# The small operands' loads of a fused decoder block, put behind its first large loads

## Chip, cores and metric

The kernel runs on one core of a Trainium2 chip. The metric is the time of one execution on the device in microseconds (us), a median over runs.

## What is computed

One decoder layer over 1024 positions of width 1024, in float32. Cut to what matters here:

```python
hn = rms_norm(h, norm1_g)
a_b, a_c, a_h, q, k, v, c_u, c_v = split(hn @ w_in)
y_a = a_b * short_conv(a_c * a_h, conv_w)
y_b = stick_breaking_attention(rms_norm(q, q_norm_g), rms_norm(k, k_norm_g), v)
y_c = spatial_gating(gelu(c_u), gelu(c_v), sgu_norm_g, sgu_w, sgu_b)
h = h + concat(y_a, y_b, y_c) @ w_out
h = h + square(relu(rms_norm(h, norm2_g) @ w_ff1)) @ w_ff2
gate = sigmoid(rms_norm(h, norm3_g) @ w_ple_gate)
h = h + gate * (p @ w_ple_proj)
```

The small operands are `norm1_g`, `norm2_g`, `norm3_g` (g1, g2, g3 in the kernel), `q_norm_g` and `k_norm_g` (gq, gk), `sgu_norm_g` (gs_b, spread over all partitions), `sgu_b` and `conv_w`. The last product, `p @ w_ple_proj`, needs nothing of the layer, so the kernel computes it first and keeps it in DRAM until the end.

## The kernel before

Every operand of a product is split into a high and a low float32r part, and a product of two operands is three matrix products (high x high, high x low, low x high; L161). ACT casts the high part, DVE (at times POOL) subtracts it from the source for the low part (`split`, L135).

The program is written as one stream; a scheduler in the framework sets the order of each engine's instructions, and an engine runs its own in order. What bears on the change is the first 45 us:

- **Loads.** Large loads are issued on SP into seven stage buffers (`stage`, L64). SP issues the next one when a buffer is free, that is, when ACT and DVE have made its parts. The first ones are two halves of pT, each with the first 384 columns of w_ple_proj, then two more of pT, then the rest of w_ple_proj, then blocks of xT and w_vu in turn.
- **Small loads.** `load_const` (L119) issues a load of a small operand on POOL. All eight stand at the start of the program: L124 to L130 and L543 to L546.
- **First products** (L675 to L686). Eight results `pp` of 128 x 1024, each in two halves; a half is six matrix products into one PSUM bank (`pp_ps`). There are two pools of two banks, one for the first halves and one for the second (`wide_bank`, L88). ACT copies a first half out, DVE a second half. POOL then issues the store of the whole result into DRAM (L686). The results lie in four buffers (tag `wt`, L680), so result 4 goes where result 0 was, once result 0's store has landed, and result 6 where result 2 was.
- **Scaling of x** (`normalize`, L217). Block k of xT is scaled by a column of g1: the high part by ACT (L141), the low part by DVE (L142). ACT squares the block as well (L182). This runs beside the first products.
- **Next products** (`gating`, L548). `vu_ps` takes the next bank in turn after the sixteen halves, the one that held the first half of result 6.

POOL's transfers are counted on eight semaphores that are used in turn (DMASW0 to DMASW7). POOL waits, ahead of an issue, until the transfer that used the same semaphore before has landed.

L1057 to L1065 hold an older use of pacing: a copy of two columns on POOL (`pace`) which waits for a tile, with issues placed behind it.

Of the kernel before, what the change touches and what calls it, by code (L numbers as in the profile page):

```python
# [7 lines left out]
F32 = mybir.dt.float32  # L8
# [5 lines left out]
P = 128  # L14
T = 1024
D = 1024
KT = D // P
# [15 lines left out]
def hybrid_block(ctx: ExitStack, tc: tile.TileContext, a: dict):  # L33
# [5 lines left out]
    nc = tc.nc  # L39
    PSUM = bass.MemoryType.PSUM  # L40

    const = ctx.enter_context(tc.tile_pool(name="const", bufs=1))
# [14 lines left out]
    def name(s):  # L57
        n_of[0] += 1
        return f"{s}_{n_of[0]}"

    def slot(s, dt=F32, shape=(P, HT)):
        return sp.tile(list(shape), dt, tag="slot", name=name(s))

    def stage(src, cols=HT, queue=nc.sync):  # L64
        t = stp.tile([P, HT], F32, tag="stage", name=name("stage"))[:, :cols]
        queue.dma_start(t, src)
        return t
# [11 lines left out]
    def half_tmp(s, shape=(P, 256)):  # L79
        return tp.tile(list(shape), F32, tag="half", name=name(s), bufs=3)  # L80

    def bank(pool, s):
        return pool.tile([P, HT], F32, tag=pool.name, name=name(s))
# [11 lines left out]
    def block(t):  # L95

        return t // 4, slice(t % 4 * P, (t % 4 + 1) * P)
# [21 lines left out]
    def load_const(key, shape):  # L119
        t = const.tile(list(shape), F32, name=f"c_{key}")  # L120
        nc.gpsimd.dma_start(t, a[key])
        return t

    g1 = load_const("g1", [P, KT])  # L124
    g2 = load_const("g2", [P, KT])
    g3 = load_const("g3", [P, KT])
    minus_g3 = const.tile([P, KT], F32, name="minus_g3")
    nc.vector.tensor_scalar_mul(minus_g3, g3, -1.0)
    gq = load_const("gq", [P, 1])
    gk = load_const("gk", [P, 1])  # L130


    last_hi, last_power = [None], [None]
# [1 line left out]
    def split(src, hi, lo, scale=None, low=nc.vector):  # L135

        if scale is None:
            last_hi[0] = nc.scalar.copy(hi, src)  # L138
            low.tensor_tensor(out=lo, in0=src, in1=hi, op=ALU.subtract)  # L139
        else:  # L140
            nc.scalar.activation(hi, src, AF.Copy, scale=scale)  # L141
            nc.vector.scalar_tensor_tensor(out=lo, in0=src, scalar=scale, in1=hi,  # L142
                                           op0=ALU.mult, op1=ALU.subtract)

    def load_w(src, cols, low=nc.vector):

        st = stage(src, cols)
        hi = wp.tile([P, 384], F32R, tag="w", name=name("whi"))
        lo = wp.tile([P, 384], F32R, tag="w", name=name("wlo"))
        split(st, hi[:, :cols], lo[:, :cols], low=low)  # L150
        return hi, lo
# [9 lines left out]
    def product(ps, terms, first=True, last=True):  # L161


        for i, ((lh, ll), (rh, rl)) in enumerate(terms):
            nc.tensor.matmul(ps, lh, rh, start=first and i == 0, stop=False)  # L165
            nc.tensor.matmul(ps, lh, rl, start=False, stop=False)  # L166
            done = nc.tensor.matmul(ps, ll, rh, start=False, stop=last and i == len(terms) - 1)  # L167
        return done

    def cols(parts, sl):  # L170
        return parts[0][:, sl], parts[1][:, sl]

    def power_mhalf(out, in_, n):
        last_power[0] = nc.gpsimd.tensor_tensor(out=out, in0=in_, in1=mhalf[:, :n], op=ALU.pow)  # L174
# [42 lines left out]
    def normalize(h):  # L217
        for k in range(KT):
            xt = stage(a["xT"][k * P:(k + 1) * P, half[h]])
            xn[k][h] = pair("xn")  # L220
            split(xt, *xn[k][h], scale=g1[:, k:k + 1])
            square_sum(S1[h], xt, k == 0, nc.vector)
            yield 1
# [19 lines left out]
    def later(units, piece):  # L243

        waiting.append((emitted[0] + units, piece))

    def stream(*gens):
        for g in gens:
            for units in g:
                emitted[0] += units  # L250
                yield units
                while waiting and waiting[0][0] <= emitted[0]:
                    units = waiting.pop(0)[1]()
                    emitted[0] += units
                    yield units
        while waiting:
            yield waiting.pop(0)[1]()
# [85 lines left out]
    def project(pr):  # L343

        wk = [load_w(a["w_qkv"][pr, k], 384, nc.gpsimd if pr and k % 2 == 0 else nc.vector)
              for k in range(KT)]

        QS = [[None, None], [None, None]]

        KH = [[None, None], [None, None]]  # L350
        KL = [[None, None], [None, None]]
        V = [None] * 4
        heads[pr] = QS, KH, KL, V
        for t in range(KT):
            th, ts = block(t)
            if t % 4 == 0:
                for hh, other in enumerate((hi_p, lo_p)):
                    KL[hh][th] = slot("KL", F32R)
                    nc.gpsimd.memset(KL[hh][th][other].bitcast(F32), 0.0)
                for hh in range(2):  # L360
                    QS[hh][th] = slot("QS", F32R)
                    KH[hh][th] = slot("KH", F32R)
            ps = bank(ps_mm, "qkv_ps")[:, :384]
            for k0 in range(0, KT, 2):
                product(ps, [(cols(xn[k][th], ts), wk[k]) for k in (k0, k0 + 1)],
                        k0 == 0, k0 == KT - 2)
                yield 18

            sq = half_tmp("qk_sq", (P, 4, HD + 1))
            nc.scalar.copy(sq[:, :, HD], ms1e[t].broadcast_to([P, 4]))  # L370
            nc.scalar.activation(sq[:, :, :HD], ps[:, :256].rearrange("p (h d) -> p h d", d=HD),
                                 AF.Square, scale=HD ** -0.5)
            ss = small.tile([P, 4], F32, tag="ss", name=name("ss"))
            nc.vector.tensor_reduce(out=ss, in_=sq, axis=AX.X, op=ALU.add)  # L374
            rs = small.tile([P, 4], F32, tag="rs", name=name("rs"))
            power_mhalf(rs, ss, 4)
            if t % 2 == 0:
                qk = tp.tile([P, 2, 256], F32, tag="qk", name=name("qk"), bufs=2)
            nc.vector.tensor_tensor(
                out=qk[:, t % 2].rearrange("p (h d) -> p h d", d=HD),  # L380
                in0=ps[:, :256].rearrange("p (h d) -> p h d", d=HD),
                in1=rs.unsqueeze(2).broadcast_to([P, 4, HD]), op=ALU.mult)
            if t % 2 == 0:
                V[t // 2] = slot("V", F32R, (P, 2, 2, 2, HD))
            v = V[t // 2][:, t % 2]
            split(ps[:, 256:].rearrange("p (h d) -> p h d", d=HD), v[:, :, 0], v[:, :, 1], scale=r1[t])
            if t % 2 == 1:
                later(72, lambda t=t, qk=qk: turn_qk(heads[pr], t, qk))
# [151 lines left out]
    ATTEND = 2 * (72 + 8 * 10 + 72 + 10 * 10 + 80)  # L540


    gs_b = const.tile([P, 256], F32, name="gs_b")  # L543
    nc.gpsimd.dma_start(gs_b, a["sgu_g"].partition_broadcast(P))
    sgb = load_const("sgu_b", [P, 4])
    cw = load_const("conv_w", [P, 2, 3])  # L546

    def gating():  # L548
        wsT = slot("wsT", shape=(P, 4, P))
        nc.sync.dma_start(wsT, a["sgu_wT"])  # L550
# [111 lines left out]
    wple = []  # L662
# [7 lines left out]
    for c0, n in UNITS[1:]:  # L670
        for k in range(2):
            wple[k].append(load_w(a["w_ple_proj"][k * P:(k + 1) * P, c0 * P:(c0 + n) * P], n * P))
    vu_parts = []
    first_half = normalize(0)
    for n in range(KT):  # L675
        next(first_half)
        st = stage(a["w_vu"][n])
        vu_parts.append(pair("vu"))
        split(st, *vu_parts[n])
        pp = at.tile([P, T], F32, tag="wt", name=name("pp"), bufs=4)  # L680
        for h in range(2):
            ps = wide_bank("pp_ps")
            product(ps, [(cols(wple[k][n // 3], slice(n % 3 * P, (n % 3 + 1) * P)), p_parts[k][h])
                         for k in range(2)])
            (nc.vector.tensor_copy if h else nc.scalar.copy)(pp[:, half[h]], ps)
        nc.gpsimd.dma_start(pp_dram[n], pp)  # L686
    for _ in normalize(1):
        pass
    alone = stream(gating(), project(0))
    fill = stream(project(1), project(2), project(3), convolve())  # L690

# [362 lines left out]


    g_sums = dram.tile([4, 4, P, HT], F32, name="g_sums")
    pace = const.tile([P, 2], F32, name="pace")  # L1057
    def gate_sums(i, behind):

        if not 0 <= i < 16:  # L1060
            return
        paced = nc.gpsimd.tensor_copy(pace, behind[:, :2])
        with tc.issue_after(paced.ins):
            block_step(i % 4, lambda to: g_sums[to, i // 4],
                       lambda of: w_block("w_ple_gate", of, i // 4), nc.gpsimd)  # L1065

# [275 lines left out]
```

## Time and profile before

| | us |
|---|---|
| median of 3 runs | 1219.47 (1216.49 to 1220.53) |
| the profiled execution, its time | 1217.19 |
| its span, first to last instruction | 1215.2 |
| PE busy | 1188.7 (98%) |
| DVE busy | 885.7 (73%) |
| ACT busy | 641.6 (53%) |
| POOL busy | 400.5 (33%) |

Times in the trace count from the start of the span. A row of the timeline has the start, the duration, engine, line, operation and tiles, and in brackets how long the engine was idle before it and what ended that. PE is TensorE, DVE VectorE, ACT ScalarE, POOL GpSimd, SP SyncE. Tiles' names leave out numbers, so c_g is g1, g2 or g3. The median lies 2.28 us above the profiled execution, so a difference is reckoned against that execution's own time.

### The profile page before, as it was taken

Reading aid. Unit: us, or ns where it says so; the run is one execution under the profiler, and the core shown is the slowest. Engines: PE = TensorE matmul, PEld = TensorE weight load, DVE = VectorE, ACT = ScalarE, POOL = GpSimd, SP = SyncE. Lnnn points to the kernel's source line nnn. Section 1 sums busy time; section 2 is a strip of 40 time slices with the busy share of each in tenths; the row PEclk is TensorE's granted clock in tenths of the full one; section 3 lists DMA queues with packets and bytes.
Section 4 is the critical chain, followed back from the end, with each engine's and each line's share of the span. In section 5 each row is a group of like instructions: output and inputs, shape, how many; then the busy total and the mean of one; then the engine's idle time right before and its main releaser. Section 6 shows DMA issues by size and latency. Waiting matters only on the chain.

```text
span 1215.2 us, 17769 instructions
## 1 busy us (share of the span) xinstructions
PE 1188.7 (98%) x5852; PEld 1015.5 (84%) x5852; DVE 885.7 (73%) x1302; ACT 641.6 (53%) x1284; POOL 400.5 (33%) x408
## 2 busy tenths in 40 slices
PE   8999999999999999999999999999999999999997
PEld 7899999898878888888888888888888888888886
DVE  7846888888787757877877777787665557753597
ACT  7737777777654355743334343355443444546542
POOL 2324456465342312124553544421023301013412
PEclk9999999999999999999999999999999999999999
DMA  9703359898653786779989989778889985654857
GB/s 300 239 18 102 115 175 278 233 197 160 145 116 79 166 286 194 207 194 266 258 242 271 239 246 264 210 255 273 320 248 314 278 264 170 216 165 108 185 158 208
DMA packets 127964, 254.04 MB, mean 209 GB/s; under 512 B 14496, under 2 KB 22432, under 8 KB 127168
## 3 DMA queue, kind: packets, MB, share of 16 engines
q1 hardware_dynamic: 94992, 168.08, 41.7%
q0 software_dynamic: 27664, 57.05, 25.3%
q10 hardware_dynamic: 5216, 27.79, 6.3%
q8 instruction: 46, 0.75, 0.3%
q14 instruction: 46, 0.38, 0.1%
HBM read 192.30 MB, written 92.80 MB: 235 GB/s over the span
## 4 chain that ended last, share of the span: by engine, by line
PE 84%; DVE 6%; DMA 3%; ACT 3%; issue 2%; POOL 1%; ACTq 0%; SPq 0%; DVEq 0%; POOLq 0%
PE f_ps L811 25%; PE d_ps L811 25%; PE g_ps L811 6%; PE qkv_ps L165 3%; PE qkv_ps L167 3%; PE qkv_ps L166 3%; PE av L494 2%; PE w_tr L476 2%; DVE rem L451 2%; PE vu_ps L167 1%; PE vu_ps L165 1%; PE vu_ps L166 1%; PE o_ps L167 1%; PE o_ps L165 1%; PE o_ps L166 1%
## 5 line engine op out<-in xcount | busy, mean ns | idle before, releaser
L139 DVE TENSOR_TENSOR w_lo<-raw,w_hi 128x512 fp32r<-128x512 f32 x280 | 241.4, 865 | 87.0 <-ACT w_hi L138 85.1
L138 ACT CAST w_hi<-raw 128x512 fp32r<-128x512 f32 x280 | 171.9, 619 | 231.5 <-PE d_ps L811 114.0
L811 PE MATMUL f_ps<-hn_hi,w_hi 128*128 128x512 f32 x448 | 175.2, 392 | 0.0
L811 PE MATMUL f_ps<-hn_hi,w_lo 128*128 128x512 f32 x448 | 174.8, 391 | 0.0
L811 PE MATMUL f_ps<-hn_lo,w_hi 128*128 128x512 f32 x448 | 174.8, 390 | 0.0
L811 PE MATMUL d_ps<-f_hi,w_hi 128*128 128x512 f32 x448 | 174.8, 390 | 0.0
L811 PE MATMUL d_ps<-f_hi,w_lo 128*128 128x512 f32 x448 | 174.3, 389 | 0.0
L811 PE MATMUL d_ps<-f_lo,w_hi 128*128 128x512 f32 x448 | 174.3, 389 | 0.0
L451 DVE TENSOR_TENSOR_SCAN rem<-rem 128x128 f32<-128x128 f32 (+3 forms) x64 | 87.6, 1376 | 19.5 <-ACT rem L446 18.8
L811 PEld LDWEIGHTS f_ps<-hn_lo,w_hi 128*128 128x128 f32 x448 | 84.5, 189 | 17.9 <-issue 0.2
L811 PEld LDWEIGHTS f_ps<-hn_hi,w_hi 128*128 128x128 f32 x448 | 84.5, 189 | 17.9 <-issue 0.2
L811 PEld LDWEIGHTS f_ps<-hn_hi,w_lo 128*128 128x128 f32 x448 | 84.4, 188 | 17.6
L811 PEld LDWEIGHTS d_ps<-f_lo,w_hi 128*128 128x128 f32 x448 | 84.1, 188 | 17.6 <-issue 0.2
L811 PEld LDWEIGHTS d_ps<-f_hi,w_lo 128*128 128x128 f32 x448 | 84.1, 188 | 17.6
L811 PEld LDWEIGHTS d_ps<-f_hi,w_hi 128*128 128x128 f32 x448 | 84.1, 188 | 17.6 <-issue 0.2
L165 PE MATMUL qkv_ps<-whi,xn_hi 128*128 128x384 f32 x256 | 89.6, 350 | 6.8 <-DVE V L142 6.8
L166 PE MATMUL qkv_ps<-wlo,xn_hi 128*128 128x384 f32 x256 | 86.7, 339 | 0.0
L167 PE MATMUL qkv_ps<-whi,xn_lo 128*128 128x384 f32 x256 | 86.6, 338 | 0.0
L139 DVE TENSOR_TENSOR f_lo<-raw,f_hi 128x512 fp32r<-128x512 f32 x112 | 78.1, 728 | 10.1 <-ACT f_hi L138 9.9
L138 ACT CAST f_hi<-raw 128x512 fp32r<-128x512 f32 x112 | 67.1, 620 | 26.0 <-DMA raw<-f_dram 20.9
L797 POOL TENSOR_TENSOR S<-S,sq 128x512 f32<-128x512 f32 x19 | 25.6, 1345 | 160.2 <-ACT sq L873 160.2
L174 POOL TENSOR_TENSOR rs<-ss,mhalf 128x4 f32<-128x4 f32 x32 | 47.5, 1484 | 68.1 <-DVE ss L374 67.3
(247 smaller groups left out, 2707.9 us busy)
## 6 DMA issues: line engine op xcount, KB each, us to landing
raw<-in_w_ff SPq DMA_DIRECT2D x148, 256.0 KB, 4.1
raw<-f_dram SPq DMA_DIRECT2D x112, 256.0 KB, 5.1
raw<-w_sums SPq DMA_DIRECT2D x64, 256.0 KB, 3.7
f_dram<-f SPq DMA_DIRECT2D x48, 256.0 KB, 4.1
f_dram<-t SPq DMA_DIRECT2D x48, 256.0 KB, 3.7
w_sums<-in_w_ff POOLq DMA_DIRECT2D x8, 1024.0 KB, 12.2
w_sums<-w_sums POOLq DMA_DIRECT2D x8, 1024.0 KB, 12.4
raw<-in_w_out SPq DMA_DIRECT2D x28, 256.0 KB, 3.7
```

What stands on the lines that cost most here:

```text
L138: last_hi[0] = nc.scalar.copy(hi, src)
L139: low.tensor_tensor(out=lo, in0=src, in1=hi, op=ALU.subtract)
L165: nc.tensor.matmul(ps, lh, rh, start=first and i == 0, stop=False)
L166: nc.tensor.matmul(ps, lh, rl, start=False, stop=False)
L167: done = nc.tensor.matmul(ps, ll, rh, start=False, stop=last and i == len(terms) - 1)
L174: last_power[0] = nc.gpsimd.tensor_tensor(out=out, in0=in_, in1=mhalf[:, :n], op=ALU.pow)
L451: nc.vector.tensor_tensor_scan(out=back, data0=back, data1=back, initial=1.0, op0=ALU.mult, op1=ALU.bypass)
L476: nc.tensor.transpose(tr[:, n:n + P], wts[i][:, kb * P:(kb + 1) * P], ident)
L494: nc.tensor.matmul(av[:, first * P:], lhs, part[:, o:o + m], start=kb == 0 and part is hi, stop=kb == 2 * g + 1 and part is lo)
L797: return eng.tensor_tensor(out=out, in0=x, in1=y, op=ALU.add)
L811: done = nc.tensor.matmul(bank, l, r, start=first and k == 0 and i == 0, stop=k == len(b) - 1 and i == 2, skip_group_check=True)
```

## The change

The loads of the small operands leave the start of the program. A helper `once` puts a copy of two columns of a given tile on POOL, which waits until that tile is written, and issues what stands under it behind that copy. The load of g1 stands behind the second high part of w_ple_proj; the other seven stand behind result 2 of the first products. The sign change of g3 moves behind the scaling of x, and the older pacing uses the same helper.

```diff
-    g1 = load_const("g1", [P, KT])
-    g2 = load_const("g2", [P, KT])
-    g3 = load_const("g3", [P, KT])
-    minus_g3 = const.tile([P, KT], F32, name="minus_g3")
-    nc.vector.tensor_scalar_mul(minus_g3, g3, -1.0)
-    gq = load_const("gq", [P, 1])
-    gk = load_const("gk", [P, 1])
+    pace = const.tile([P, 2], F32, name="pace")
+
+    def once(behind):
+
+        return tc.issue_after(nc.gpsimd.tensor_copy(pace, behind[:, :2]).ins)
...
-    gs_b = const.tile([P, 256], F32, name="gs_b")
-    nc.gpsimd.dma_start(gs_b, a["sgu_g"].partition_broadcast(P))
-    sgb = load_const("sgu_b", [P, 4])
-    cw = load_const("conv_w", [P, 2, 3])
...
+    with once(wple[1][0][0].bitcast(F32)):
+        g1 = load_const("g1", [P, KT])
...
+        if n == 2:
+            with once(pp):
+                gs_b = const.tile([P, 256], F32, name="gs_b")
+                nc.gpsimd.dma_start(gs_b, a["sgu_g"].partition_broadcast(P))
+                sgb = load_const("sgu_b", [P, 4])
+                gq = load_const("gq", [P, 1])
+                gk = load_const("gk", [P, 1])
+                g2 = load_const("g2", [P, KT])
+                g3 = load_const("g3", [P, KT])
+                cw = load_const("conv_w", [P, 2, 3])
         nc.gpsimd.dma_start(pp_dram[n], pp)
     for _ in normalize(1):
         pass
+    minus_g3 = const.tile([P, KT], F32, name="minus_g3")
+    nc.vector.tensor_scalar_mul(minus_g3, g3, -1.0)
```

How the orders stand, with the semaphores that a row waits for. On POOL, from the last of its early own work to the third result's store (pp_61 is result 2), before:

```order
L114 AFFINE_SELECT below_104<-below_104 128x128 [waits Pool_49]
L121 DMA c_g3_115<-in_g3 128x8
L121 DMA c_gq_119<-in_gq 128x1
L121 DMA c_gk_121<-in_gk 128x1
L544 DMA gs_b_131<-in_sgu_g 128x256
L121 DMA c_sgu_b_133<-in_sgu_b 128x4
L121 DMA c_conv_w_135<-in_conv_w 128x6
L686 DMA pp_dram_137<-pp_41_211 128x1024 [waits DMASW0_49,DVE_49,Activation_49]
L686 DMA pp_dram_137<-pp_51_244 128x1024 [waits DMASW1_49,DVE_49,Activation_49]
L686 DMA pp_dram_137<-pp_61_277 128x1024 [waits DMASW2_49,DVE_49,Activation_49]
```

and now, from the load of g1 on (whose pacing copy stands ahead of it, behind the work of L114):

```order
L121 DMA c_g1_182<-in_g1 128x8
L692 DMA pp_dram_120<-pp_41_197 128x1024 [waits DVE_49,Activation_49]
L692 DMA pp_dram_120<-pp_51_230 128x1024 [waits DVE_49,Activation_49]
L128 COPY pace_111<-pp_61_263 128x2 [waits Activation_49,Pool_49]
L685 DMA gs_b_281<-in_sgu_g 128x256
L121 DMA c_sgu_b_283<-in_sgu_b 128x4
L121 DMA c_gq_285<-in_gq 128x1
L121 DMA c_gk_287<-in_gk 128x1
L121 DMA c_g2_289<-in_g2 128x8
L121 DMA c_g3_291<-in_g3 128x8 [waits DMASW0_49]
L121 DMA c_conv_w_293<-in_conv_w 128x6 [waits DMASW1_49]
L692 DMA pp_dram_120<-pp_61_263 128x1024 [waits DMASW2_49,DVE_49]
```

The store of result 2 stood directly behind that of result 1 and waited for g3's landing (DMASW2). Seven loads now stand between the two; conv_w waits for the store of result 0 (the one that used DMASW1 before it), and the store of result 2 for that of result 1.

On ACT, around the copy of result 6's first half (pp_101), before:

```order
L141 ACTIVATE xn_hi_85_363<-stage_84_361,c_g1_111 128x512
L685 COPY pp_101_409<-pp_ps_102_410 128x512 [waits DVE_49,DMASW2_49,PE_49,Activation_49]
L138 CAST vu_hi_89_372<-stage_88_370 128x512 [waits DMAHW5_49]
L182 ACTIVATE sq_97_400<-stage_94_394 128x512 [waits DMAHW6_49]
L141 ACTIVATE xn_hi_95_396<-stage_94_394,c_g1_111 128x512
L685 COPY pp_111_442<-pp_ps_112_443 128x512 [waits DVE_49,DMASW3_49,PE_49,Activation_49]
L138 CAST vu_hi_99_405<-stage_98_403 128x512 [waits DMAHW7_49]
L141 ACTIVATE xn_hi_105_429<-stage_104_427,c_g1_111 128x512 [waits DMAHW0_49]
```

and now:

```order
L139 ACTIVATE xn_hi_95_397<-stage_94_395,c_g1_182 128x512
L180 ACTIVATE sq_107_434<-stage_104_428 128x512 [waits DMAHW0_49,DVE_49]
L136 CAST vu_hi_99_406<-stage_98_404 128x512 [waits DMAHW7_49]
L139 ACTIVATE xn_hi_105_430<-stage_104_428,c_g1_182 128x512
L681 COPY pp_101_410<-pp_ps_102_411 128x512 [waits DVE_49,DMASW2_49,PE_49,Pool_49]
L136 CAST vu_hi_109_439<-stage_108_437 128x512 [waits DMAHW1_49]
L139 ACTIVATE xn_hi_115_463<-stage_114_461,c_g1_182 128x512 [waits DMAHW2_49]
```

The copies of results 6 and 7 have moved behind the scaling (xn_hi_105) and square of the eighth block, which are the last of the first half of x. On PE, result 7's second half (pp_ps_113), which stood behind 13 products of vu, now stands ahead of all of vu:

```order
L167 MATMUL pp_ps_103_418<-p_hi_21_170,wlo_34_195 128x512
L165 MATMUL vu_ps_148_537<-vu_hi_39_207,xn_hi_36_200 128x512 [waits Activation_49]
L166 MATMUL vu_ps_148_537<-vu_lo_40_208,xn_hi_36_200 128x512
L167 MATMUL vu_ps_148_537<-vu_hi_39_207,xn_lo_37_201 128x512
L165 MATMUL vu_ps_148_537<-vu_hi_49_240,xn_hi_45_231 128x512
```

This was before (the last product of result 6, then vu), and now:

```order
L165 MATMUL pp_ps_113_452<-p_hi_18_147,wlo_31_172 128x512
L163 MATMUL pp_ps_113_452<-p_hi_21_153,whi_33_177 128x512
L164 MATMUL pp_ps_113_452<-p_lo_22_154,whi_33_177 128x512
L165 MATMUL pp_ps_113_452<-p_hi_21_153,wlo_34_178 128x512
L163 MATMUL vu_ps_148_540<-vu_hi_39_193,xn_hi_36_186 128x512 [waits Activation_49]
```

The first vu product waits for ACT in both, and what it waits for is the copy that frees its bank. From about the second vu result on, the order of every engine is the same as before.

More of the change, by code (lines that the diff above doesn't have):

```diff
@@ L1056, in hybrid_block @@
     g_sums = dram.tile([4, 4, P, HT], F32, name="g_sums")
-    pace = const.tile([P, 2], F32, name="pace")
     def gate_sums(i, behind):
@@ L1061, in gate_sums @@
             return
-        paced = nc.gpsimd.tensor_copy(pace, behind[:, :2])
-        with tc.issue_after(paced.ins):
+        with once(behind):
             block_step(i % 4, lambda to: g_sums[to, i // 4],
```

## The prediction

> **What bounds the kernel now.** I read the page first, then the waits of PE, then the stretches by engine, and last the first 35 us in order of time.
>
> ```profile
> span 1215.2 us, 17769 instructions
> PE 1188.7 (98%) x5852; PEld 1015.5 (84%) x5852; DVE 885.7 (73%) x1302; ACT 641.6 (53%) x1284; POOL 400.5 (33%) x408
> ```
>
> PE is the bound: of 1215.2 us it is idle for 26.5. A change among the first loads can only win back PE's idle time near the start. The waits of PE in the first 130 us (total, times, longest) and the busy time of each engine in three stretches say how much that is:
>
> ```profile
> PE pp_ps L165 <- ACT whi L138: 2.5, 1, 2.5
> PE qkv_ps L165 <- DVE V L142: 1.2, 1, 1.2
> 4.50:8.70 4.20, 1.78 (x8) 1.16 (x7) 1.32 (x3) 1.15 (x3) 2.00 (x4) 1.00 0.96 276
> 8.70:28.00 19.30, 19.26 (x85) 15.96 (x86) 17.56 (x31) 16.33 (x31) 2.67 (x5) 1.00 0.97 330
> 28.00:58.00 30.00, 30.00 (x141) 25.01 (x139) 26.72 (x54) 24.56 (x47) 10.19 (x10) 1.00 0.79 274
> ```
>
> There is one gap of 2.5 us, between 4.5 and 8.7, and then none until 58. In the second stretch 85 products take 19.26 us, so one product of 512 columns takes 0.2266 us; I use that below. The gap in order of time (start, duration, idle before):
>
> ```profile
> 1.46 0.68 POOL L121 DMA_DIRECT2D c_g<-in_g  x1
> 5.67 0.61 PE L167 MATMUL pp_ps<-p_hi,wlo 128*128 128x512 f32 x2
> 5.97 0.53 POOL L121 DMA_DIRECT2D c_conv_w<-in_conv_w  x1
> 7.53 0.62 ACT L138 CAST p_hi<-stage 128x512 fp32r<-128x512 f32 x1 [3.00 <-DMA stage<-in_pT]
> 8.18 0.51 ACT L138 CAST whi<-stage 128x384 fp32r<-128x384 f32 x1
> 8.74 0.73 PE L165 MATMUL pp_ps<-p_hi,whi 128*128 128x512 f32 x2 [2.46 <-ACT whi L138]
> ```
>
> PE ends its first six products at 6.28 and waits for the second weight part, which ACT casts from 8.18 to 8.69. ACT had waited 3.00 us for the third load. The first load (issued in the stretch 0.5 to 1.2), the third (1.7 to 2.15) and the chain's row of the fourth, with their times to landing:
>
> ```profile
> stage<-in_pT SPq DMA_DIRECT2D x1, 256.0 KB, 2.7
> ...
> stage<-in_pT SPq DMA_DIRECT2D x1, 256.0 KB, 5.8
> ...
> 2.19 5.97 DMA stage<-in_w_ple_proj
> ```
>
> So the third and fourth loads took 5.8 and 6.0 us where the first took 2.7. POOL issues its eight small loads from 1.46 to 6.50, in just this stretch.
>
> **The eight small loads leave the start.** POOL's issue time costs nothing, before or after: POOL has no other work on the path there. What matters is how much their transfers hold up the large ones. The queues' shares of the 16 engines from 3.5 to 8.2 (q0 is POOL's, q1 SP's), and then from 12 to 16, where q0 carries nothing:
>
> ```profile
> q1 hardware_dynamic: 671, 1.11, 87.1%
> q0 software_dynamic: 112, 0.02, 4.3%
> ...
> GB/s 287 389 410 389 328 328 348 389 348 348 287 164 184 143 123 205 164 82 143 123 225 164 184 164 205 225 287 225 266 369 328 328 369 430 410 430 348 389 307 307
> q1 hardware_dynamic: 614, 1.11, 93.5%
> ```
>
> The least gain is 0.043 x 4.7 = 0.20 us, the time that small packets hold the engines. The most is the whole gap, 2.46: were the fourth load to land after 2.7 us (at 4.9), its cast would end by 5.4, ahead of PE's 6.28. A loss is excluded, since nothing is put ahead of these loads. Between these ends I stay near the lower one: from 12 to 16 SP's queue alone falls to 82 to 225 GB/s for over 1 us, so the loads have slow spells that no small load causes. I take **0.7 us gained**.
>
> [...]
>
> **The load of g1 comes later, just ahead of its first use.** The first use on ACT, a small copy like the new one on POOL, the landing of the first and of the slowest of the three g loads, and a copy out of PSUM on ACT:
>
> ```profile
> 12.69 0.72 ACT L141 ACTIVATE xn_hi<-stage,c_g 128x512 fp32r<-128x512 f32 x1
> L1062 POOL COPY pace<-h x12: 184/514/581, 891.7 to 973.5; 128x2 f32<-128x2 f32 x12
> c_g<-in_g POOLq DMA_DIRECT2D x1, 4.0 KB, 4.6
> ...
> c_g<-in_g POOLq DMA_DIRECT2D x1, 4.0 KB, 6.4
> ...
> 16.03 0.57 ACT L685 COPY pp<-pp_ps 128x512 f32<-128x512 f32 x1
> ```
>
> On the clock of before: the weight part is written at 8.69, the pacing copy takes 0.51, so the issue begins at 9.2 and g1 lands 4.6 to 6.4 later, at 13.8 to 15.6. The scaling at 12.69 wants it, so ACT is held for 1.1 to 2.9 us. Behind it on ACT are the cast of a weight part, two squares, casts, and the copy at 16.03 (third result, first half) that frees a bank. PE asks for that bank after 42 more products, at 8.74 + 42 x 0.2266 = 18.26; the copy ends at 16.60. So 1.66 us of lateness are covered by the PE products of results 0 to 3, and only 0 to 1.2 us can reach PE. I take **0**: 1.1 is the likelier landing.
>
> [...] If ACT did not catch up, that would be rival C.
>
> **The other seven loads stand ahead of the third result's store.** This is where I see the price. Rows: three stores on POOL as issued now, the first two's time to landing (stretches 14 to 15 and 15 to 16), all eight's, then ACT's copy of result 6 and PE's first vu product:
>
> ```profile
> 14.16 0.54 POOL L686 DMA_DIRECT2D pp_dram<-pp  x1 [7.66 <-ACT whi L138]
> 15.74 0.54 POOL L686 DMA_DIRECT2D pp_dram<-pp  x1 [1.04 <-ACT sq L182]
> 19.56 0.53 POOL L686 DMA_DIRECT2D pp_dram<-pp  x1 [3.28 <-ACT vu_hi L138]
> pp_dram<-pp POOLq DMA_DIRECT2D x1, 512.0 KB, 7.1
> ...
> pp_dram<-pp POOLq DMA_DIRECT2D x1, 512.0 KB, 7.8
> ...
> DMA to landing us min/median/max: 6.2/6.6/7.8
> 27.00 0.56 ACT L685 COPY pp<-pp_ps 128x512 f32<-128x512 f32 x1
> 27.91 0.39 PE L165 MATMUL vu_ps<-vu_hi,xn_hi 128*128 128x512 f32 x1
> ```
>
> POOL's row now: second pacing copy (waits for ACT's half of result 2, 16.60), five issues of 0.54 that wait for nothing, g3 (waits for g1's landing), conv_w (waits for the landing of store 0: 14.16 + 7.1 = 21.26), and only then store 2, which waits for the landing of store 1: 15.74 + 7.8 = 23.54. So store 2 slips from 19.56 to 23.54. With 6.2 to 7.8 to land it is done at 29.74 to 31.34, median 30.14. Four buffers hold the results, so ACT's copy of result 6 goes into the buffer of result 2 and waits for that; with 0.56 for the copy the bank is free at 30.7. PE's first vu product takes that bank. PE itself comes to it after all results: eight of two halves of six products, 96 less the first six, so 8.74 + 90 x 0.2266 = 29.13 (result 7's second half, now ahead of vu, included). That makes a stall of 1.6 us, where before there was none: the copy ended at 27.56 and PE went on at 27.91. Everything in this paragraph moves along with whatever the first loads gain, so the stall doesn't shrink with that gain.
>
> ACT has its own way to the same copy, since its row now puts the last scaling and square of the first half ahead of it. From two rows of now and ACT's total wait for xT between 10 and 40:
>
> ```profile
> 30.54 0.72 ACT L141 ACTIVATE xn_hi<-stage,c_g 128x512 fp32r<-128x512 f32 x1
> 31.16 0.62 ACT L182 ACTIVATE sq<-stage 128x512 f32<-128x512 f32 x1
> ACT sq L182 <- DMA stage<-in_xT: 2.9, 4, 1.2
> ```
>
> The scaling ends at 31.26; two copies of 0.56 that stood ahead now stand behind, the square of 0.62 stands ahead: 31.26 - 1.12 + 0.62 = 30.76, so the copy would end at 31.3 and the stall be 2.2. Held-back stores leave the loads more of the engines, and up to 2.9 us of waiting could go, so this way may be shorter. The ends: no stall, if store 2, alone in its queue, lands like the first load (23.54 + 2.7); and 31.34 + 0.56 - 29.13 = 2.8. I take **1.8 us lost**, between the two ways.
>
> No cost elsewhere. The moved operands are used far behind: the earliest, gs_b, at 47.7. The sign change of g3 moves on DVE behind a scaling of the sixth block; it takes 0.16 us, and DVE is not what PE waits for there.
>
> ```profile
> L614 DVE TENSOR_TENSOR vu<-vu,gs_b x8: 409/420/426, 47.7 to 79.8; 128x256 f32<-128x256 f32 x8
> 11.37 0.16 DVE L128 TENSOR_SCALAR minus_g<-c_g 128x8 f32<-128x8 f32 x1
> ```
>
> From there on the instructions stand as before, and PE, the bound, carries any shift to the end.
>
> **Sum.** -0.7 + 0 + 1.8 = +1.1 us. The profiled execution took 1217.19 us with a span of 1215.2, so it should become 1218.3 and 1216.3. The median of the three runs, 1219.47, lies 2.28 above that execution; on it the forecast is 1220.6.
>
> **The rivals.**
>
> - A, the forecast (0.50): small gain at the start, stall at the first vu product. 1220.6.
> - B (0.30): the small loads do hold up the first ones, and the whole gap of 2.46 goes. For it: 5.8 and 6.0 us against 2.7, while the small loads are in flight. Against it: their 4.3%. With the stall of 1.8 that gives -0.7, 1218.8; without a stall -2.46, 1217.0. More than 2.46 is not there to be had.
> - C, the other side (0.13): g1 lands 2.9 us late and ACT, which does the casts, the scalings and half of the copies, does not catch up. Stage buffers then come free late, loads slip with them, and the copy of result 6 ends at 31.3 + 2.9 = 34.2: a stall of 5.1, 1224.6. It becomes decisive once more than 1.5 us of lateness remain at that copy, for then 2.2 + 1.5 passes 3.66. Against it: ACT waits 2.9 us for loads in this stretch, time in which it could catch up.
> - D (0.07): the order is changed, yet neither effect is seen: the first loads land as before and store 2 is early enough. 1219.5.
>
> **How the numbers follow.** About 0.3%, 3.66 us, is what a measurement of this kernel can tell from no change; the three runs themselves span 4.04. A, B and D all lie inside it. Only B's end without a stall together with a low run would read as faster: 0.04. C and a tail of A make slower: 0.14. The rest, 0.82, is no change. The range goes from B's end, 1217.0, up to the loss with no gain, a stall of 2.8 and part of the 1.2 that g1 can cost (+3.5): 1223.0.
>
> **What would show it.** Step one: times to landing of the third and fourth load (5.8, 6.0) and PE's wait before 8.74; a fall below 4 us and a wait under 1 us prove B. Step two: ACT's idle time before the first scaling, ended by the load of g1, about 1 us. Step three: store 2's issue about 8 us behind store 1's, and a PE wait of 1.6 to 2.2 us at the first vu product, ended by ACT's copy of result 6. If that wait is missing, or follows something else, step three is wrong. If the end moves by more than the start does, what I say of everything behind 30 us is wrong.

## The result, and the profile after

| | before | after |
|---|---|---|
| median of 20 runs each, us | 1218.38 (1213.7 to 1222.24) | 1222.07 (1216.57 to 1228.05) |
| profiled execution: time, span | 1217.19, 1215.2 | 1220.75, 1218.7 |
| PE busy | 1188.7 | 1189.9 |

The ratio is 1.0036 with an interval of 1.0022 to 1.0050: the change makes the kernel slower, by 2.7 to 6.1 us. The forecast was +1.1 us, no measurable change; the outcome is the one that had been given 0.14, though the medians, 3.69 us apart, only just pass the 3.66 us that the prediction set for it.

The waits of PE in the first 130 us after the change (total, times, longest) show a new first row:

```profile
PE vu_ps L163 <- ACT pp L681: 3.6, 1, 3.6
PE pp_ps L163 <- ACT whi L136: 1.6, 1, 1.6
PE qkv_ps L163 <- DVE V L140: 1.2, 1, 1.2
```

The gap before the second half of the first products is 1.6 instead of 2.5, and a gap of 3.6 at the first vu product is new. Both in order of time, with POOL's pacing copy and issues between them:

```profile
6.24 0.62 ACT L136 CAST p_hi<-stage 128x512 fp32r<-128x512 f32 x1 [1.83 <-DMA stage<-in_pT]
...
7.17 0.51 ACT L136 CAST whi<-stage 128x384 fp32r<-128x384 f32 x1 [0.32 <-DMA stage<-in_w_ple_proj]
...
7.73 0.73 PE L163 MATMUL pp_ps<-p_hi,whi 128*128 128x512 f32 x2 [1.62 <-ACT whi L136]
...
8.26 0.70 POOL L121 DMA_DIRECT2D c_g<-in_g  x1
...
11.20 0.72 ACT L139 ACTIVATE xn_hi<-stage,c_g 128x512 fp32r<-128x512 f32 x1
...
14.51 0.54 POOL L692 DMA_DIRECT2D pp_dram<-pp  x1 [1.01 <-ACT sq L180]
...
15.50 0.39 POOL L128 COPY pace<-pp 128x2 f32<-128x2 f32 x1 [0.45 <-ACT pp L681]
...
22.22 1.18 POOL L692 DMA_DIRECT2D pp_dram<-pp  x2 [2.48 <-DVE S L181]
...
28.04 0.39 PE L165 MATMUL pp_ps<-p_hi,wlo 128*128 128x512 f32 x1
...
29.74 0.63 ACT L180 ACTIVATE sq<-stage 128x512 f32<-128x512 f32 x1 [1.80 <-DMA stage<-in_xT]
...
30.28 0.60 ACT L136 CAST vu_hi<-stage 128x512 fp32r<-128x512 f32 x1
...
30.79 0.72 ACT L139 ACTIVATE xn_hi<-stage,c_g 128x512 fp32r<-128x512 f32 x1
...
31.41 0.56 ACT L681 COPY pp<-pp_ps 128x512 f32<-128x512 f32 x1
...
32.03 0.80 PE L163 MATMUL vu_ps<-vu_hi,xn_hi 128*128 128x512 f32 x1 [3.60 <-ACT pp L681]
```

The third load is used at 6.24 (7.53 before), and PE's second half begins 1.01 us earlier. The first scaling, at 11.20, has no idle time before it: g1, issued at 8.26, took 2.9 us to land and was there just in time. The third result's store is issued 7.7 us behind the second's. PE ends the first products at 28.43. ACT is idle until the load of the first half's last block lands at 29.7; square, a cast and the scaling follow, and only then, at 31.41, the copy that frees PE's bank.

The gap has a second price, the granted clock: the share of its full clock that PE was given. The busy times of each engine in four stretches (after the length: PE's busy time and count first; the last three numbers are the granted clock, the DMA share and GB/s):

```profile
27.91:31.32 3.41, 0.52 (x3) 0.09 (x1) 1.80 (x4) 1.61 (x4) 0.00 (x0) 1.00 1.04 383
31.32:34.73 3.41, 2.70 (x6) 2.15 (x7) 3.30 (x6) 2.48 (x6) 0.53 (x1) 0.50 1.01 350
34.73:38.14 3.41, 3.41 (x9) 2.64 (x8) 3.15 (x6) 3.41 (x7) 0.53 (x1) 0.50 1.04 372
38.14:41.55 3.41, 3.41 (x16) 2.82 (x15) 0.27 (x1) 1.54 (x3) 0.00 (x0) 1.00 0.75 284
```

Behind the stretch in which PE worked for 0.52 us only, the clock is at 0.50 for two stretches of 3.41 us, with 6 and 9 products where the next, at full clock, has 16. Counting PE's products from the start, the one behind the gap starts 2.75 us later than in before (less than 3.60, since PE came 1.01 earlier), and from 38.14 on they come 5.74 later: the clock takes 3.0 us in this execution.

### The profile page after: what moved, and what is told of

It is laid out like the page before. It is cut to its first block, busy times and chain, and to the rows that moved or that the text cites. A ratio compares the mean times of both kernels' runs of the same rounds, so it can differ in the third digit from the quotient of the medians.

```text
span 1218.7 us, 17770 instructions
## 1 busy us (share of the span) xinstructions
PE 1189.9 (98%) x5852; PEld 1016.4 (83%) x5852; DVE 881.0 (72%) x1302; ACT 641.1 (53%) x1284; POOL 404.4 (33%) x410
## 4 chain that ended last, share of the span: by engine, by line
PE 81%; DVE 7%; ACT 4%; DMA 3%; issue 3%; POOL 1%; ACTq 0%; SPq 0%; DVEq 0%; POOLq 0%
PE f_ps L819 25%; PE d_ps L819 25%; PE g_ps L819 6%; DVE rem L449 2%; PE o_ps L165 2%; PE o_ps L163 2%; PE o_ps L164 2%; PE qkv_ps L163 2%; PE qkv_ps L165 2%; PE qkv_ps L164 2%; PE cv_ps L163 2%; PE cv_ps L164 2%; PE cv_ps L165 2%; PE av L492 1%; PE vu_ps L163 1%
## 5 line engine op out<-in xcount | busy, mean ns | idle before, releaser
L137 DVE TENSOR_TENSOR w_lo<-raw,w_hi 128x512 fp32r<-128x512 f32 x280 | 246.0, 882 | 87.1 <-ACT w_hi L136 85.0
L819 PEld LDWEIGHTS d_ps<-f_hi,w_lo 128*128 128x128 f32 x448 | 84.1, 188 | 17.4
L805 POOL TENSOR_TENSOR S<-S,sq 128x512 f32<-128x512 f32 x19 | 27.4, 1440 | 158.4 <-ACT sq L881 158.4
```

The costliest lines, as they stand in the source:

```text
L805: return eng.tensor_tensor(out=out, in0=x, in1=y, op=ALU.add)
L819: done = nc.tensor.matmul(bank, l, r, start=first and k == 0 and i == 0, stop=k == len(b) - 1 and i == 2, skip_group_check=True)
```

## The experiments

Each experiment was run in 7 to 12 executions beside 23 to 35 of before on the same chip, unless another count stands with it. Besides the times I use a second measure. For every run the span and the mean granted clock are known, and a stretch at 0.50 does about half the work (6 and 9 products above, where the next has 16). So span times clock estimates the span that the run would have had at full clock, and 2 x (1 - clock) x span is the time at half speed. For before this gives 1208.3 us in each of the three sessions (25, 35 and 23 runs), with 13.4, 14.7 and 15.9 us at half speed. In all twelve profiles 3.2 to 6.8 us of the time at half speed lie at the very end, behind PE's last product, as here after the change, with PE at 0.00 us busy:

```profile
1212.33:1218.73 6.40, 0.00 (x0) 0.00 (x0) 1.62 (x4) 0.04 (x1) 0.00 (x0) 0.50 0.24 87
```

So the measure serves for differences between kernels, not as a time that could be reached. A single figure in brackets behind a mean, or behind a difference of means, is its standard error.

**1. The seven loads last.** They stand behind the last result's two columns.

```diff
-        if n == 2:
+        nc.gpsimd.dma_start(pp_dram[n], pp)
+        if n == KT - 1:
             with once(pp):
                 gs_b = const.tile([P, 256], F32, name="gs_b")
...
-        nc.gpsimd.dma_start(pp_dram[n], pp)
```

> The seven loads stand behind the last result's two columns instead of the third's; g1 stays where the change puts it. Theory (the loss comes from the seven loads, which put ACT's copy of result 6 behind the last load's square and scaling): PE's wait of 3.60 us at the first vu product falls to 0.3 or less, its granted clock stays 1.0 from 28 to 45 us (0.50 from 31.63 to 38.45 in the changed kernel), the gap before the second half of the first products stays 1.6, and the time is 1.0 us below before (-0.1%). Rival 1 (g1's late landing delays ACT): a wait of 2 us or more stays at the first vu product, and the time is 2 to 5 us above before. Rival 2 (the clock falls there for reasons of its own): no wait, yet 0.50 for some 7 us, and the time is 2 us above before.

ACT's copy of result 6, and PE from the last first product to the first vu product:

```profile
25.56 0.59 ACT L681 COPY pp<-pp_ps 128x512 f32<-128x512 f32 x1
...
26.81 0.39 PE L165 MATMUL pp_ps<-p_hi,wlo 128*128 128x512 f32 x1
27.03 0.39 PE L163 MATMUL vu_ps<-vu_hi,xn_hi 128*128 128x512 f32 x1
```

The copy no longer stands behind the last block's scaling, and PE goes on without a wait; the clock stays 1.0 there. Ratio 1.0009 (0.9997 to 1.0021), at full clock 1208.0 (0.3), 0.3 below before. So the loss hangs on the place of the seven. The gain of 1.0 is not there in the times, though PE was 0.88 us ahead of before in the trace; experiment 8 tells why.

**2. Four of the seven there.** gs_b, sgu_b, gq and gk stay behind result 2, so that no store waits for a landing; g2, g3 and conv_w go last.

```diff
                 gk = load_const("gk", [P, 1])
+        nc.gpsimd.dma_start(pp_dram[n], pp)
+        if n == KT - 1:
+            with once(pp):
                 g2 = load_const("g2", [P, KT])
...
-        nc.gpsimd.dma_start(pp_dram[n], pp)
```

> Only gs_b, sgu_b, gq and gk are loaded behind the third result; g2, g3 and conv_w follow behind the last. The third store then waits for no landing. Theory (what costs is the wait of conv_w and of the third store for earlier stores to land, and the order on ACT that follows from it): the third store is issued before 20 us (22.22 in the changed kernel), PE waits 0.3 us or less at the first vu product, no fall of the clock there, time 1.0 us below before. Rival 1 (small loads among the large ones slow these, whatever their semaphores): the load of the last block still lands at 29.5 or later and PE waits 1.5 to 3 us. Rival 2 (g1's late landing): a wait of 2 us or more.

```profile
18.95 0.54 POOL L689 DMA_DIRECT2D pp_dram<-pp  x1
...
27.45 0.62 ACT L136 CAST vu_hi<-stage 128x512 fp32r<-128x512 f32 x1 [1.22 <-DMA stage<-in_w_vu]
27.97 0.58 ACT L681 COPY pp<-pp_ps 128x512 f32<-128x512 f32 x1
...
28.60 0.50 PE L163 MATMUL vu_ps<-vu_hi,xn_hi 128*128 128x512 f32 x1 [1.12 <-ACT pp L681]
```

The store goes out at 18.95, yet PE waits 1.12: now the copy stands behind a cast that waits 1.22 us for its load. That load is not late: it lands at 27.4, and in before's first profile at 27.7, but there the copy, at 27.00, stood ahead of the cast. Ratio 1.0023 (1.0012 to 1.0035), at full clock 1209.6 (0.5). My theory of waits for landings is half right: without them the stall is smaller, but it doesn't go. In this kernel as in the changed one, what ends last is a load that ACT's order puts ahead of the copy. Whether small loads slow the large ones here can't be read from one profile.

**3. The copy first.** The changed kernel, with the last block's scaling and square put behind the copy of result 6.

```diff
-        next(first_half)
+        if n == KT - 1:
+            with tc.issue_after(copied.ins):
+                next(first_half)
+        else:
+            next(first_half)
...
+            if h == 0:
+                copied = done
```

> The changed kernel, with ACT's scaling and square of the first half's last block put behind its copy of result 6. Theory (ACT's order holds the copy from 28.2, when the third store lands, to 31.41): the copy starts at about 28.3, PE's wait at the first vu product falls from 3.60 to 0.5 to 0.9 us and is ended by that copy, the granted clock stays 1.0 (a gap of 1.62 us before 7.73 left it at 1.0), and the time is 0.3 us below before, 5 below the changed kernel. Rival (the third store's landing alone sets it): the copy starts at 30 us or later, the wait stays above 2.5 us.

```profile
22.50 0.54 POOL L698 DMA_DIRECT2D pp_dram<-pp  x1 [2.13 <-DMA pp_dram<-pp]
...
29.07 0.58 ACT L685 COPY pp<-pp_ps 128x512 f32<-128x512 f32 x1
...
29.71 0.50 PE L163 MATMUL vu_ps<-vu_hi,xn_hi 128*128 128x512 f32 x1 [0.74 <-ACT pp L685]
```

POOL's row, the seven loads and the late store are those of the changed kernel; only ACT's order differs. The wait falls from 3.60 to 0.74, the clock stays 1.0. Ratio 1.0013 (1.0003 to 1.0023), at full clock 1208.5 (0.2), where the changed kernel has 1211.6 to 1212.3. So ACT's order carries nearly the whole stall; the store's landing costs at most the 0.74. The time expected, 0.3 us below before, was missed: the mean is 0.9 above, of which 0.2 is left at full clock.

**4. The gap filled.** 14 products more on PE between the last of the first products and the first vu product.

```diff
+            last = product(ps, [(cols(wple[k][n // 3], slice(n % 3 * P, (n % 3 + 1) * P)), p_parts[k][h])
...
+    with tc.issue_after(last.ins):
+        fill_ps = bank(ps_tr, "fill")
+        for i in range(14):
+            nc.tensor.matmul(fill_ps, wple[0][2][0][:, :P], p_parts[0][0][0], start=True, stop=True)
     for _ in normalize(1):
```

> The changed kernel with 14 products more (of parts that are there already, their result unused) on PE between the last of the first products and the first vu product: 14 x 0.2266 = 3.2 us of work in the gap of 3.60. Theory (the fall of the clock to 0.50 for 6.83 us is caused by PE's gap): the first vu product starts at about 32.0 as in the changed kernel, the clock stays 1.0, the products behind it take 0.227 each, and from the second vu result on PE is 2.6 us behind before instead of 5.7; time 2.6 above before, 3.1 below the changed kernel. Rival (the clock falls for another reason, say the work done since the start): it falls there all the same, and PE is 5.7 us behind before.

```profile
27.75 3.33 PE L696 MATMUL fill<-p_hi,whi 128*128 128x512 f32 x14
31.60 0.50 PE L163 MATMUL vu_ps<-vu_hi,xn_hi 128*128 128x512 f32 x1 [0.51 <-ACT pp L681]
```

The first vu product comes nearly as late as in the changed kernel, the clock stays 1.0 behind it, and PE's products come 2.5 us later than in before where the changed kernel's come 5.7 later, as expected. But the time was 1.0045 (1.0031 to 1.0059) of before in 6 runs, no better than the changed kernel in its own session. That left open how the loss splits; experiments 9 and 10 take it up on one chip.

**5. The order alone.** The kernel before, with all small loads at the start; only the copy of result 6 is put behind the last block's scaling.

```diff
+        if n == KT - 1:
+            with tc.issue_after(last_hi[0].ins):
+                nc.scalar.copy(held[0][:, half[0]], held[1])
+            nc.gpsimd.dma_start(pp_dram[n - 1], held[0])
...
+            if h == 0 and n == KT - 2:
+                held = pp, ps
```

> The kernel before, with all small loads at the start; only ACT's copy of result 6 (and that result's store) is put behind the scaling of the first half's last block, where the changed kernel has it. Theory (the place of that copy on ACT makes the stall): that block's load landed at 28.4 in before, its scaling and square then end at 29.8, the copy at 30.3; PE is done with the first products at 29.1 and waits 1.2 us or more at the first vu product, more where the load lands later; with a wait under 1.9 us the clock stays 1.0, with one over 2.5 it falls to 0.50 for one or two stretches of 3.41 us. PE is 1.2 to 6 us behind before from the second vu result on, and so is the time. Rival (the seven loads themselves, their traffic or the wait of the third store, make the stall): no wait at the first vu product, time as before.

```profile
28.21 0.72 ACT L141 ACTIVATE xn_hi<-stage,c_g 128x512 fp32r<-128x512 f32 x1 [0.49 <-DMA stage<-in_xT]
28.84 0.61 ACT L182 ACTIVATE sq<-stage 128x512 f32<-128x512 f32 x1
29.36 0.56 ACT L692 COPY pp<-pp_ps 128x512 f32<-128x512 f32 x1
...
29.98 0.50 PE L165 MATMUL vu_ps<-vu_hi,xn_hi 128*128 128x512 f32 x1 [1.11 <-ACT pp L692]
...
31.50 0.57 ACT L679 COPY pp<-pp_ps 128x512 f32<-128x512 f32 x1
```

This is a weaker counterproof than meant. The copy of result 6 came at 31.50, but the scheduler gave the first vu product the other bank, that of result 7, whose copy (29.36) stood behind the seventh block's scaling and square. PE waits 1.11 us with every small load at the start, so ACT's order alone makes a stall. (The 28.4 of the expectation is the landing of the seventh block's load; the eighth's lands at 29.7 in before, see experiment 9.) In time it is lost in the noise: 0.9994 (0.9981 to 1.0007); at full clock 1209.3 (0.3), 1.0 above before, and PE's products come 0.84 later than in before's first profile. The 1.2 to 6 us expected are not there.

**6. g1 at the start, seven last** (these as in experiment 1). **7. g1 alone**: before, with only g1 paced. Their edits for g1:

```diff
+    g1 = load_const("g1", [P, KT])
     pace = const.tile([P, 2], F32, name="pace")
...
-    with once(wple[1][0][0].bitcast(F32)):
-        g1 = load_const("g1", [P, KT])
```

```diff
-    g1 = load_const("g1", [P, KT])
...
+    paced = nc.gpsimd.tensor_copy(pace, wple[1][0][0].bitcast(F32)[:, :2])
+    with tc.issue_after(paced.ins):
+        g1 = load_const("g1", [P, KT])
```

> The load of g1 at the start as in before, the other seven behind the last result. Theory (g1's own place costs and gains nothing; the gain at the start comes from the seven): the third load lands by 6.5, PE's gap before the second half of the first products is 1.6 to 1.9, no wait at the first vu product, PE 0.8 to 1.0 ahead of before from 10 us on, and the time the same as with the seven last and g1 paced (1217.6 beside 1216.9 of before), within 1.2 us. Rival (any small load among the first ones holds them): the gap is 2.4 as in before. Rival 2 (g1's pacing costs): time 1 us or more below that of the seven last with g1 paced.

> The kernel before with one thing changed: g1 loaded behind the pacing copy. Theory (g1's place does nothing): PE's gap stays 2.3 to 2.5, ACT is not idle for g1 by more than 0.3 us ahead of its first scaling, no wait at the first vu product, time as before within 1.2 us. Rival (g1 comes late and ACT doesn't catch up): ACT idle by 1 us or more for g1, PE waits 1 us or more among the first products or at the first vu product, time 1 to 5 us above before.

With g1 at the start the gap is 1.70, the ratio 1.0004 (0.9990 to 1.0017), at full clock 1208.3 (0.3): the same as experiment 1 within the noise. With g1 alone the ratio is 1.0007 (0.9993 to 1.0021), at full clock 1209.1 (0.3). Here "does nothing" was too much said:

```profile
8.30 1.15 PE L164 MATMUL pp_ps<-p_hi,whi 128*128 128x512 f32 x2 [1.92 <-ACT whi L137]
...
17.53 0.73 ACT L140 ACTIVATE xn_hi<-stage,c_g 128x512 fp32r<-128x512 f32 x1
...
29.80 0.50 PE L164 MATMUL vu_ps<-vu_hi,xn_hi 128*128 128x512 f32 x1 [0.55 <-ACT pp L688]
```

ACT never idles for g1, but the scheduler puts the first scaling at 17.53, behind copies and squares. The stage buffers come free late (SP issues no load between 13.46 and 19.82), loads follow late, and PE waits 0.55. It is an effect of the order, not of the load's landing, and the changed kernel hasn't got it (scaling at 11.20). The clock falls here as well, to 0.50 behind the gap of 1.92 (last section).

**8. Before once more.**

> The kernel before once more, unchanged, in the place of a changed one. It shows what the comparison makes of no change. If the 0.1 to 0.2% by which the kernels with the seven loads last or the copy first came out above before are chance in the runs of before, this one shows a ratio of 1.000 with an interval of about 0.0012 to either side, and its fall of the clock (0.50 for 3.41 us near 283, 340 or 527 us) stands in other places than in the first profile of before, with PE's gap of 2.5 us at 282 half inside one stretch of 3.41 us or cut by its end.

```profile
5.27 0.73 PE L165 MATMUL pp_ps<-p_hi,whi 128*128 128x512 f32 x2 [0.58 <-ACT whi L138]
6.71 0.62 ACT L138 CAST p_hi<-stage 128x512 fp32r<-128x512 f32 x1 [1.49 <-DMA stage<-in_pT]
7.83 0.73 PE L165 MATMUL pp_ps<-p_hi,whi 128*128 128x512 f32 x2 [0.90 <-ACT whi L138]
```

The ratio is 1.0001 (0.9988 to 1.0014). The trace is the surprise. With all eight small loads at the start PE's second half begins at 7.83, 0.91 earlier than in the first profile of before and hardly later than after the change (7.73). The gap of 2.46 on which I had built was in good part one execution's. Over all profiles this product begins at 8.74, 8.30, 8.02 and 7.83 with seven or eight small loads at the start (mean 8.22), at 8.03 with one, and at 8.14, 8.02, 7.85, 7.76, 7.74, 7.73 and 7.19 with none (mean 7.78). So some 0.4 us may be gained, with overlapping values; at full clock experiment 1 has 0.3 (0.4) and experiment 6 none. The fall of the clock moved only in part, against the expectation: it is near 339 us in both profiles of before, near 527 in the first alone, and near 282 in neither.

**9. The changed kernel, and 10. the filled gap, once more on one chip.** No edits to those above. In the first expectation the span at full clock is simply s x c.

> The changed kernel once more, unchanged, beside the next one and runs of before on the same chip. Open is how the loss splits into PE's wait at the first vu product and the fall of the clock behind it. For each run the mean granted clock c and the span s are known; s less half of the time at half speed, s(2c - 1)/1 worked out as s - (1 - c)s, is the span that the run would have had at full clock. Theory: so worked out it is 3.5 to 4.5 us above before's (1212.3 beside 1208.3 in the runs so far), that is, most of the loss is the wait, and 1 to 1.5 us more come from 2 to 3 us more at half speed. The profile shows a wait of 3 to 5 us at the first vu product ended by ACT's copy of result 6, behind the square and scaling of the last block. Rival (the wait of 3.60 was one execution's chance): a wait under 2 us, and a span at full clock within 1.5 us of before's.

> The changed kernel with 14 more products in PE's gap, once more, on the same chip as the changed kernel itself. Theory: at full clock its span is that of the changed kernel within 0.7 us, since the products lie in the wait; its time at half speed is 2 us shorter or more, since no stretch of 3.41 us near 30 us is idle for the most part; so it takes 1 us less or more. Rival (what follows the gap costs nothing in the mean, since the clock falls somewhere else in its place): the same time at half speed, the same time as the changed kernel.

| | ratio to before | mean time | at full clock | at half speed |
|---|---|---|---|---|
| before | | 1218.2 (0.4) | 1208.3 (0.2) | 15.9 (0.6) |
| changed | 1.0039 (1.0026 to 1.0053) | 1222.8 (0.6) | 1211.6 (0.3) | 18.5 (1.1) |
| changed, gap filled | 1.0027 (1.0014 to 1.0039) | 1221.4 (0.6) | 1212.0 (0.4) | 14.4 (1.0) |

The first row is of 23 runs, the others are of 12. The changed kernel loses 4.6 us: 3.3 (0.4) at full clock, a little under the 3.5 to 4.5 expected, and (18.5 - 15.9) / 2 = 1.3 (0.6) by the clock. Filling the gap gives back 4.1 (1.5) us at half speed, 1.4 (0.8) us of time, and nothing at full clock. One session alone leaves the clock's share uncertain. The earlier 20 runs of the changed kernel have 1212.3 and 16.7, and all runs whose clock is known give 14.6 (0.3) us at half speed for 95 of before, 17.4 (0.7) for 32 of the changed kernel and 14.5 (0.8) for 18 with the gap filled: the clock's share is then (17.4 - 14.6) / 2 = 1.4 (0.4), and nothing of it is left with the gap filled. The profile of experiment 9 has the same two rows as the first, with a wait somewhat under the 3 to 5 us expected:

```profile
29.75 0.63 ACT L180 ACTIVATE sq<-stage 128x512 f32<-128x512 f32 x1 [1.50 <-DMA stage<-in_xT]
...
32.03 0.50 PE L163 MATMUL vu_ps<-vu_hi,xn_hi 128*128 128x512 f32 x1 [2.70 <-ACT pp L681]
```

and its gap lies in two stretches of the clock's grid (columns as above):

```profile
27.20:30.61 3.41, 2.13 (x9) 1.17 (x7) 3.02 (x6) 1.91 (x4) 0.53 (x1) 1.00 1.02 346
30.61:34.03 3.42, 2.00 (x9) 1.66 (x10) 3.11 (x6) 3.42 (x7) 0.53 (x1) 1.00 1.03 395
34.03:37.40 3.37, 3.37 (x17) 2.79 (x16) 3.37 (x7) 3.30 (x7) 0.53 (x1) 1.00 1.04 408
```

The gap of 2.70 is shared by two stretches, PE is busy for 0.62 and 0.58 of them, and the clock stays 1.00, where the expectation of experiment 5 had it fall for a wait of over 2.5. That bound was an estimate: until then PE's longest gaps in the first 35 us had been 1.62 (after the change), 1.79 (experiment 1) and 2.46 (before) with the clock at 1.00 behind them, and 3.60 (after the change) with 0.50.

The vu product starts at 32.03 as in the first profile, although PE arrived 0.9 us later this time: the load sets its time, not PE. (That the two agree to the hundredth is chance: with the same order on ACT the copy ends at 31.55 in experiment 4 and at 31.28 in 10.) Here is the issue on SP of this load, the eighth block's, with its time to landing, in before and after the change:

```profile
23.40 0.33 SPq L66 DMA_DIRECT2D stage<-in_xT  x1
stage<-in_xT SPq DMA_DIRECT2D x1, 256.0 KB, 6.3
...
22.72 0.33 SPq L66 DMA_DIRECT2D stage<-in_xT  x1
stage<-in_xT SPq DMA_DIRECT2D x1, 256.0 KB, 6.9
```

It lands at 29.7 in both, and in experiment 9 too (24.59 + 5.1). In before the copy of result 6 stood ahead of it on ACT; after the change the copy stands behind it. In ten of the profiles this load lands between 28.7 and 29.8: at 29.5 in the mean of the five with the seven loads ahead of it, at 29.4 in the mean of the five without, so no delay by the seven is seen there. Nor does it follow PE: the mean is 29.4 both in the five where PE is 0.88 to 1.55 us ahead of before and in the five where it is 0 to 0.72 ahead. The other two profiles have 34.3 (experiment 7, where it is issued only at 29.50) and 31.8 (experiment 2, with four of the small loads ahead of it, issued at 23.94 as in the others), so a delay by small loads is not excluded.

## Why the prediction was right in its mechanism and wrong in its size

- **First loads, -0.7.** The profile pair shows -1.01, experiment 8 that most of this is the spread of single executions; some 0.4 us or less remain. The estimate was of the right order; rival B's 2.46 was not there to be had, and that gap did not repeat (0.58 and 0.90 in experiment 8).
- **g1, 0.** Right in its worth: no idle time at the first scaling. But g1 took 2.9 us to land and not the 4.6 to 6.4 of the loads at the start, so the hold of 1.1 us on ACT was not seen; in experiment 1, where it took 3.7, ACT was idle for 0.73 us and PE did not feel it. Rival C's mechanism did not occur, though the time came out on its side. The issue of g1 at 8.26 was just early enough for the use at 11.20.
- **Stall at the first vu product, +1.8.** The place, the cause and the releaser are as forecast: PE's wait ended by ACT's copy of result 6, the third store issued 7.7 us behind the second's. Of the two ways ACT's own row counted and not the store (experiment 3). Its size failed, 3.60 and 2.70 against 1.8. The first step that failed is "31.26 - 1.12 + 0.62": I took two copies' time off a row of ACT as if only ACT's work set it. That puts the scaling of the eighth block at 29.42, ahead of the load that it needs, which landed at 29.7 in the trace of before already (experiment 9). With square, cast and scaling behind that landing the copy ends at 31.97, not 31.3.
- **"Everything in this paragraph moves along with whatever the first loads gain".** This is the second step that failed. PE came 1.0 us earlier, the load did not: it lands at 29.7 in both, and from its issue to its landing the DMA share is 1.04 in before and 1.03 after. So the microsecond gained at the start was spent as a longer wait, and the sum of -0.7 and +1.8 had added two terms that are one: the first vu product starts when the copy ends, forecast at 30.9 less the gain of 0.7, measured at 32.03.
- **"No cost elsewhere".** Wrong by some 1.3 us in the mean: the clock was at 0.50 for 6.83 us behind the gap of 3.60, and stayed 1.00 behind that of 2.70 (experiment 9).
- **Sum.** Forecast +1.1; measured 3.3 at full clock in experiment 9 (4.0 for the first 20 runs, set against 1208.3, since their own runs of before have no clock on record), and some 1.3 by the clock. That the time, 1222.07, lies inside the range of 1217.0 to 1223.0 is luck: the range was counted from the median of three runs, 1219.47, and 20 runs of before have 1218.38. The change itself, 3.69, is more than the +3.5 at the range's upper end. The chances did not foresee it: "slower" had 0.14 because the stall was bounded at 2.8 and the clock had no term at all.

What stays open: why the last block's load lands as late as 31.8 in experiment 2, whether small loads ever delay it, and how large the clock's share is to better than half a microsecond. No version tried is measurably faster than before; the seven loads last, or g1 at the start with them, are its equals.

## What to carry to other kernels

Moving DMA issues changed more than their own queue here: ACT's copy of result 6 started at 27.00 before and at 31.41 after. Look where the scheduler now puts the copy that frees PE's next bank, and which load stands ahead of it on that engine. Read the landing of that load from the trace of before, even if nothing waits for it there: it would have given some 32.0 for the copy's end here. The time that this load set, in a stretch with the DMA engines full (share 1.04 and 1.03), stayed where it was, 29.7, when the work ahead got 1.0 us faster, so a gain ahead of it and a wait at it must not be summed. Before a gap of one profile is priced, see whether a second profile of the same kernel has it.

## What the hardware showed that was not expected

In the twelve profiles the granted clock changed on a grid of 3.41 us: ahead of PE's last product every stretch at 0.50 lasted 3.41 or 6.83 us, and the two such stretches of a profile began 187.73 us apart in the first of before and 314.03 in the first after the change, 55 and 92 times 3.413. Its place against the program differed between executions of one kernel: around PE's gap a stretch begins at 27.91 in the first profile of the changed kernel and at 27.20 in that of experiment 9. Of the stretches of that grid in which PE was busy for less than 0.44, all 8 were followed by one or two at 0.50; of 38 with 0.44 to 0.61, 13 were: one near 340 us in each profile, where most have two weak stretches in a row, and the one in experiment 7 below. A gap shorter than a stretch was enough in experiment 7, 1.92 us:

```profile
4.99:8.41 3.42, 1.50 (x7) 0.92 (x6) 1.11 (x3) 1.14 (x3) 1.07 (x3) 1.00 0.92 291
8.41:11.82 3.41, 3.41 (x9) 2.63 (x10) 2.35 (x6) 2.73 (x6) 0.95 (x2) 0.50 0.94 279
```

9 products in a stretch that holds 16 at full clock, while before's gap of 2.46 (PE busy for 0.45 of its stretch) and the 2.70 above left the clock at 1.00. The falls counted here stand behind stretches that were 15 to 60% busy. Part of this kernel's spread from run to run goes with the clock: in each set of runs the spans rise by 0.2 to 0.7 us per us at half speed. In four of the profiles the clock also fell near 527 us behind stretches in which PE was fully busy; for that I have no cause.
